# Gate and up products of the feed-forward network as 2 x 2 block products, three k-tile pairs of eight with seven products, on weight blocks of four k tiles

## The chip, the cores and the metric

The kernel runs on one core of one Trainium2 chip. The metric is device time in microseconds of one execution, the median of the runs shown. Inputs and output lie in HBM; the host only lays the weights out in another order before the launch.

## What is computed

The reference is a two-layer decoder trunk over 256 tokens of width 2048 in float32: layer A has a gMLP mixer, layer B a sparse-attention mixer on a shared K/V set, and each layer goes on with a SwiGLU network and a gated per-layer embedding. What the change touches is the SwiGLU network, with an inner width of 5632:

```python
def swiglu(h, w_in, w_out):
    g, u = jnp.split(h @ w_in, 2, axis=-1)
    return (jax.nn.silu(g) * u) @ w_out
# in each of the 2 layers:
x = x + swiglu(rmsnorm(x, norm_ffn[i]), ffn_w_in[i], ffn_w_out[i])
```

## The kernel before, in words

**Number format.** Every float32 operand is split into a high part in the fp32r format and the exact rest (`split`, L81: ScalarE copies the high part, VectorE subtracts it from the source). A product of two such operands is three matmuls into one PSUM bank (`mm3`, L90: high x high L91, high x rest L92, rest x high L93). Activations are the stationary operand (128 x 128), weights the moving one (128 x 512).

**Weight stream.** `wblock` (L109) loads two k tiles by 512 columns, 512 KB, into one of four `raw` tiles on the SyncE queue and splits them into one of four pairs `wh`, `wl` (128 x 1024). `gemm_blocks` (L121) makes one step for each such block: for both token tiles and both k tiles an `mm3`, 12 matmuls. All large matrices of the kernel use this stream.

**Feed-forward.** `ffn` (L328) goes over 11 chunks of 512 inner columns in three parts (4, 4 and 3 chunks). For a chunk, `gemm` makes the gate (`g`, two PSUM banks of `ps_acc`, one for each token tile), ScalarE applies Silu to it (L338), a second `gemm` makes the up half (`u`), VectorE multiplies the two (`ac`, L342), and `mid_T` (L189) turns the result around with eight TensorE transposes (`mT`, L196) and splits it into `aT`. After each part, four `fo` products with the output matrix are added to the residual in `x_sb` (L187). I call the work of one chunk up to `aT` a unit: 2 x 16 k tiles x 2 token tiles x 3 = 192 matmuls and 8 transposes. There are 11 units in each of two layers, 22 in all.

**Activations of the feed-forward.** `x_chunk_T` (L160) transposes 512 columns of the residual after each `ao` (layer A, L311 to L322) or `bo` (layer B, L703 to L717) chunk, and splits them with the norm's gain into `hT`. The row norms are applied later, as a scale `rs` at the Silu and at the multiplication.

**Buffers.** PSUM has eight banks: four in `ps_acc` (`gemm_acc`) and four in `ps_gen` (transposes and small products). Scratch tiles `t0`, `t1`, `t2` have two buffers each.

**Order of the work.** Each engine runs its own instructions in a fixed order. That order is laid by the scheduler of the tile framework when the program is built, from the order of the source, the dependences and its own estimate of the durations; an instruction can be put ahead of one that stands earlier in the source. The SyncE queue takes the weight loads in source order; `issue_after` puts the few other loads behind them. After the `ao` chunk 2 that queue also writes a replicated bias table of 4.2 MB (`prepare_bias`, L230).

Of the kernel before, what the change touches and what calls it, by code (L numbers as in the profile page):

```python
# [17 lines left out]
TT = 2  # L18
# [31 lines left out]

@with_exitstack
def trunk_kernel(ctx: ExitStack, tc: tile.TileContext, a: dict, out: bass.AP):
# [4 lines left out]
    wp = ctx.enter_context(tc.tile_pool(name="wp", bufs=4))  # L57
# [36 lines left out]

    def gen_bank(nm):
        return ps_gen.tile([P, NC], F32, tag="gen", name=nm)

    def rsqrt_mean(dst, ss, n):
        """dst = (ss / n + EPS) ** -0.5"""
        w = ss.shape[-1]  # L100
        ms = sm.tile([P, 16], F32, tag="ms", name="ms")
        pr = ss.shape[0]
        nc.vector.tensor_scalar(ms[:pr, :w], ss, 1.0 / n, EPS, op0=ALU.mult, op1=ALU.add)
        nc.gpsimd.tensor_tensor(dst, ms[:pr, :w], neg_half[:pr, :w], ALU.pow)

# [1 line left out]
    last_load = [None]  # L107

    def wblock(src, off, n):  # L109
        raw = wp.tile([P, KT * NC], F32, tag="raw", name="raw", bufs=4)  # L110
        sz = P * KT * n
        last_load[0] = nc.sync.dma_start(raw[:, :KT * n], src[off:off + sz].rearrange("(p f) -> p f", p=P))
        wh = wp.tile([P, KT * NC], F32R, tag="wh", name="wh")
        wl = wp.tile([P, KT * NC], F32R, tag="wl", name="wl")
        split(wh[:, :KT * n], wl[:, :KT * n], raw[:, :KT * n])
        return wh, wl

    def gemm_acc(nm):
        return [ps_acc.tile([P, NC], F32, tag="acc", name=f"{nm}_{t}") for t in range(TT)]

    def gemm_blocks(accs, acth, actl, src, off, n, nk):  # L121
        """one closure for each KT k tiles of a chunk whose blocks start at element off"""
        def block(b):
            wh, wl = wblock(src, off + b * P * KT * n, n)
            for t in range(TT):
                cs = slice(t * P, (t + 1) * P)
                for j in range(KT):
                    k = b * KT + j
                    mm3(accs[t][:, :n], acth[:, k, cs], actl[:, k, cs],
                        wh[:, j * n:(j + 1) * n], wl[:, j * n:(j + 1) * n],  # L130
                        start=(k == 0), stop=(k == nk - 1))
        return [lambda b=b: block(b) for b in range(nk // KT)]

    def weave(blocks, side):
        """the blocks in order, with the side steps spread between them"""
        done = 0
        for i, blk in enumerate(blocks):
            blk()
            upto = len(side) * (i + 1) // len(blocks)
            for st in side[done:upto]:  # L140
                st()
            done = upto
# [17 lines left out]
    def x_chunk_T(dst, which, c):  # L160
        """transposed, gained and split columns of x for the next matmul"""
        hi, lo = dst
        for kk in range(0, 4, 2):
            pt = gen_bank("xT")
            for j in range(2):
                k = c * 4 + kk + j
                for t in range(TT):
                    nc.tensor.transpose(pt[:, j * SEQ + t * P:j * SEQ + (t + 1) * P],
                                        x_sb[:, t, k * P:(k + 1) * P], ident)
            for j in range(2):  # L170
                k = c * 4 + kk + j
                split(hi[:, k, :], lo[:, k, :], pt[:, j * SEQ:(j + 1) * SEQ], gain(which, k))

# [30 lines left out]
    # ================= layer A: gMLP mixer =================  # L204
# [25 lines left out]
    def prepare_bias(pool, tbl, oh):  # L230
        """bias_rep[p, h, m]: the masked bias of head h at distance 255 - m, the same for each p"""
# [11 lines left out]
    with ExitStack() as actx:  # L243
# [31 lines left out]
        for c in range(NCH):  # L275
# [7 lines left out]
            # keep s <= t (partition s, column t)  # L283
# [28 lines left out]
    hT = big_pair("h", "hF0")  # L312
    ss = new_ss()
    with tc.tile_pool(name="prep", bufs=1) as prep:
        for c in range(NCH):
            accs = gemm(f"ao{c}", gT[0], gT[1], a["a_w_out"], c * CH_D, NC, KD)
            add_to_x(accs, c)
            x_chunk_T(hT, G_FFN0, c)
# [3 lines left out]
            if c == 2:  # L322
                prepare_bias(prep, *onehot)

    def ffn(layer, hT, ss, which_next):
# [6 lines left out]
        for pi, part in enumerate(parts):  # L332
            aT = big_pair("big", f"aT{layer}_{pi}")
            for ci, c in enumerate(part):
                accg = gemm(f"g{c}", hT[0], hT[1], win, c * CH_D, NC, KD)
                sil = tp.tile([P, TT, NC], F32, tag="t0", name="sil")
                for t in range(TT):
                    nc.scalar.activation(sil[:, t, :], accg[t], AF.Silu, scale=rs[:, t:t + 1])  # L338
                accu = gemm(f"u{c}", hT[0], hT[1], win, (FCH + c) * CH_D, NC, KD)
                ac = tp.tile([P, TT, NC], F32, tag="t1", name="ac")  # L340
                for t in range(TT):
                    nc.vector.scalar_tensor_tensor(ac[:, t, :], accu[t], rs[:, t:t + 1], sil[:, t, :],  # L342
                                                   op0=ALU.mult, op1=ALU.mult)
                mid_T(aT, ci * 4, ac)
# [46 lines left out]
    rs = finish_rstd(ss2)  # L391

    # ================= shared K/V and layer B: NSA mixer =================
    with ExitStack() as bctx:
# [27 lines left out]
                # T holds for each l [high part | rest] of 30 columns: one pass gives both rows  # L422
# [56 lines left out]
        # selected and window branches: k | v  # L479
# [27 lines left out]
        # compressed branch: k_c | v_c  # L507
# [40 lines left out]
        def attn_steps(h, qh, ql, e):  # L548
            """the steps of one head; softmax rows are ordered S1 W1 S0 W0 C1 C0 (branch, token tile)"""
# [3 lines left out]
            def scores():  # L553
# [7 lines left out]
                # bias[p, c]: distance 128 + p - c; the keys of the compressed branch end 16 apart  # L561
# [18 lines left out]
                for r, (lv, sv_, bv) in enumerate(rows):  # L580
                    # lv = -(score + bias), nmx = -max(score + bias)
# [13 lines left out]
            def transposes():  # L595
# [3 lines left out]
                for b in range(2):  # L599
# [3 lines left out]
                    # only the first 16 rows of these two are used  # L603
# [81 lines left out]
        for h0, nh, n, c0 in Q_CHUNKS:  # L685
# [3 lines left out]
            # steps between the blocks of the next chunk: each finds its inputs ready  # L689
# [13 lines left out]
        hT = big_pair("h", "hF1")  # L703
        ss = new_ss()
        acc2 = [gemm_acc(f"bo{c}") for c in range(2)]
        blk2 = [gemm_blocks(acc2[c], oT[0], oT[1], a["b_w_out"], c * CH_D, NC, KD) for c in range(2)]
        weave(blk2[0][:6] + blk2[1][:6], side)
        for c in range(NCH):
            if c < 2:
                accs = acc2[c]  # L710
                for blk in blk2[c][6:]:
                    blk()
            else:
                accs = gemm(f"bo{c}", oT[0], oT[1], a["b_w_out"], c * CH_D, NC, KD)
            add_to_x(accs, c)
            x_chunk_T(hT, G_FFN1, c)
            x_chunk_stats(ss, c)  # L717
# [7 lines left out]
    ple(1, hT, ss, store)  # L725


# [1 line left out]
def _tiled(w, widths=None):  # L729
    """[K, N] -> flat: per chunk of columns, per KT k tiles, [128, KT, n]"""  # L730
# [12 lines left out]

def _buckets(dist):
    """T5 buckets of the relative positions (a table of the shapes alone)"""
# [19 lines left out]
def _layout(i):  # L765
# [35 lines left out]
    for n in ("ffn_w_in", "ffn_w_out", "ple_w", "ple_gate"):  # L801
        r[n] = np.stack([_tiled(A[n][l]) for l in range(2)])
# [18 lines left out]
```

## Time and profile before

| | us |
|---|---|
| median of 3 runs | 2315.26 |
| lowest, highest run | 2313.7, 2316.68 |
| the profiled execution, first to last instruction | 2313.6 |
| TensorE busy in it (matmuls) | 2293.5 (99%) |
| VectorE busy in it | 1267.5 (55%) |
| ScalarE busy in it | 1107.5 (48%) |

The page gives the span of the profiled execution and no other time of it; the median of the runs is 1.7 us above that span. Busy times are unions over an engine's instructions. A matmul's own duration is not its cost in a stream, since matmuls overlap; the distance from one to the next is.

### The profile page before, as it was taken

The numbers are of one execution on the slowest core, as the hardware profiler recorded it, in microseconds if no ns is written. First come the engines' busy times: TensorE is split into PE (matmuls) and PEld (weight loads), VectorE is DVE, ScalarE is ACT, GpSimd is POOL, SyncE is SP. The second block draws the span as 40 slices with busy tenths as digits, with TensorE's granted clock in tenths as the row PEclk, the third lists the DMA queues.
The fourth block names the chain that finished last, engine by engine and source line by source line (L and its number), as shares of the span: only waits on it lengthen the run. The fifth ranks groups of instructions, "written<-read, shape, count | busy, mean of one in ns | idle before, by whom it ended". The sixth has DMA issues, their size and how long they took to land.

```text
span 2313.6 us, 27764 instructions
## 1 busy us (share of the span) xinstructions
PE 2293.5 (99%) x10617; PEld 1903.5 (82%) x10617; DVE 1267.5 (55%) x1587; ACT 1107.5 (48%) x1471; POOL 23.9 (1%) x26
## 2 busy tenths in 40 slices
PE   8999999999999999999999999999999999999999
PEld 6888878888888888888887998888888888888887
DVE  5565554454454545555667776545545445444654
ACT  6554454443444344455557665544434443344543
POOL 0000000000000000000000000000000000000000
PEclk9999999999999999999999999999999999999999
DMA  8665675565655665556657344565555556555564
GB/s 291 188 194 180 214 237 190 191 191 191 191 190 184 195 195 184 190 186 187 183 176 239 114 149 137 183 196 184 190 194 190 190 191 191 192 190 191 187 197 149
DMA packets 122882, 438.63 MB, mean 190 GB/s; under 512 B 13708, under 2 KB 15884, under 8 KB 122237
## 3 DMA queue, kind: packets, MB, share of 16 engines
q1 hardware_dynamic: 121372, 434.40, 58.9%
q10 hardware_dynamic: 1296, 2.20, 0.3%
q8 instruction: 83, 1.36, 0.2%
q14 instruction: 51, 0.41, 0.1%
q0 software_dynamic: 80, 0.26, 0.0%
HBM read 434.68 MB, written 6.46 MB: 191 GB/s over the span
## 4 chain that ended last, share of the span: by engine, by line
PE 96%; DMA 2%; DVE 1%; ACT 1%; issue 0%; POOL 0%; SPq 0%; DVEq 0%; ACTq 0%
PE u L91 8%; PE u L93 8%; PE u L92 8%; PE fo L91 7%; PE fo L92 7%; PE fo L93 7%; PE g L92 7%; PE g L93 7%; PE g L91 7%; PE pg L91 2%; PE pg L93 2%; PE pg L92 2%; PE bo L91 1%; PE bo L93 1%; PE bo L92 1%; PE mT L196 1%
## 5 line engine op out<-in xcount | busy, mean ns | idle before, releaser
L85 DVE TENSOR_TENSOR wl<-raw,wh 128x1024 fp32r<-128x1024 f32 (+1 forms) x808 | 980.8, 1216 | 971.7 <-ACT wh L84 971.2
L84 ACT ACTIVATE wh<-raw 128x1024 fp32r<-128x1024 f32 (+1 forms) x808 | 849.4, 1053 | 1097.7 <-PE u L93 313.0
L91 PE MATMUL g<-wh,hF0h 128*128 128x512 f32 x352 | 137.3, 390 | 1.3 <-ACT wh L84 1.3
L92 PE MATMUL g<-wl,hF0h 128*128 128x512 f32 x352 | 137.9, 392 | 0.5 <-DVE wl L85 0.5
L92 PE MATMUL g<-wl,hF1h 128*128 128x512 f32 x352 | 137.8, 392 | 0.0
L93 PE MATMUL g<-wh,hF1l 128*128 128x512 f32 x352 | 137.8, 391 | 0.0
L93 PE MATMUL g<-wh,hF0l 128*128 128x512 f32 x352 | 137.7, 391 | 0.0
L91 PE MATMUL g<-wh,hF1h 128*128 128x512 f32 x352 | 137.2, 390 | 0.0
L91 PE MATMUL u<-wh,hF0h 128*128 128x512 f32 x352 | 136.9, 389 | 0.0
L92 PE MATMUL u<-wl,hF0h 128*128 128x512 f32 x352 | 136.9, 389 | 0.0
L93 PE MATMUL u<-wh,hF0l 128*128 128x512 f32 x352 | 136.9, 389 | 0.0
L91 PE MATMUL u<-wh,hF1h 128*128 128x512 f32 x352 | 136.9, 389 | 0.0
L92 PE MATMUL u<-wl,hF1h 128*128 128x512 f32 x352 | 136.9, 389 | 0.0
L93 PE MATMUL u<-wh,hF1l 128*128 128x512 f32 x352 | 136.9, 389 | 0.0
L93 PE MATMUL fo<-wh,aT_0l 128*128 128x512 f32 x256 | 99.8, 390 | 0.0
L93 PE MATMUL fo<-wh,aT_1l 128*128 128x512 f32 x256 | 99.8, 390 | 0.0
L92 PE MATMUL fo<-wl,aT_0h 128*128 128x512 f32 x256 | 99.8, 390 | 0.0
L92 PE MATMUL fo<-wl,aT_1h 128*128 128x512 f32 x256 | 99.8, 390 | 0.0
L91 PE MATMUL fo<-wh,aT_1h 128*128 128x512 f32 x256 | 99.6, 389 | 0.0
L91 PE MATMUL fo<-wh,aT_0h 128*128 128x512 f32 x256 | 99.6, 389 | 0.0
L91 PEld LDWEIGHTS g<-wh,hF0h 128*128 128x128 f32 x352 | 66.0, 188 | 15.2 <-ACT wh L84 1.7
L92 PEld LDWEIGHTS g<-wl,hF0h 128*128 128x128 f32 x352 | 66.1, 188 | 14.3 <-DVE wl L85 1.0
(272 smaller groups left out, 4181.2 us busy)
## 6 DMA issues: line engine op xcount, KB each, us to landing
raw<-in_ffn_w_in SPq DMA_DIRECT2D x352, 512.0 KB, 3.5
raw<-in_ffn_w_out SPq DMA_DIRECT2D x176, 512.0 KB, 3.5
raw<-in_a_w_in SPq DMA_DIRECT2D x64, 512.0 KB, 4.0
raw<-in_ple_gate SPq DMA_DIRECT2D x64, 512.0 KB, 3.6
raw<-in_a_w_out SPq DMA_DIRECT2D x32, 512.0 KB, 3.6
raw<-in_b_w_out SPq DMA_DIRECT2D x32, 512.0 KB, 3.5
raw<-in_kv_w SPq DMA_DIRECT2D x24, 512.0 KB, 3.7
raw<-in_b_w_in SPq DMA_DIRECT2D x24, 384.0 KB, 3.5
```

The source lines that it names most:

```text
L84: nc.scalar.activation(hi, src, AF.Copy)
L85: nc.vector.tensor_tensor(lo, src, f32v(hi), ALU.subtract)
L91: nc.tensor.matmul(ps, lh, rh, start=start, stop=False)
L92: nc.tensor.matmul(ps, lh, rl, start=False, stop=False)
L93: nc.tensor.matmul(ps, ll, rh, start=False, stop=stop)
L196: nc.tensor.transpose(pt[:, j * SEQ + t * P:j * SEQ + (t + 1) * P], src[:, t, (kk + j) * P:(kk + j + 1) * P], ident)
```

## The change

The gate and up halves of one chunk are made together in `ffn_unit`. For a pair of k tiles (a, b), the activations of the two token tiles form a 2 x 2 block matrix, and the four weight blocks (up and gate of k tiles a and b) another. In five pairs of eight (0, 1, 3, 5, 7), the eight block products are kept. In pairs 2, 4 and 6 Strassen's scheme (Winograd's form) takes seven products, of sums of the blocks. Products gather over all pairs in seven PSUM banks (four of `ps_acc`, three of `ps_gen`), and the gate and up chunks are sums of these banks. So that plain pairs can use the same banks, one token tile's product with the up half takes the difference of the activations (`extra`).

The weight of a pair, 1 MB, is now one block. `ffn_w_in` is laid out so on the host (`_paired`). The weight stream is opened anew for stretches: narrow as before, or wide, with blocks of four k tiles (128 x 2048) in three buffers of each kind. It is wide from `ao` to the end of the first embedding step and from the last quarter of `bo` chunks 0 and 1 to the end. It is narrow in the gMLP's first matrix and in the attention.

```diff
+NPAIR = KD // 2
+PAIRS7 = (2, 4, 6)
...
-    wp = ctx.enter_context(tc.tile_pool(name="wp", bufs=4))
...
+    def open_stream(wide):
+        cur["sb"] = es = ExitStack()
+        cur["kt"] = 2 * KT if wide else KT
+        cur["nblk"] = 0
+        for nm in ("raw", "wh", "wl"):
+            cur[nm] = es.enter_context(tc.tile_pool(name="w_" + nm, bufs=2 if wide else 4, reuse_waits="tile"))
+        cur["third"] = es.enter_context(tc.tile_pool(name="w_third", bufs=1, reuse_waits="tile")) if wide else None
+        return es
...
+    def x_chunk_forms(dst, which, c):
+        hi, lo, exh, exl = dst
+        for j in (2 * c, 2 * c + 1):
...
+            f = tp.tile([P, 8, P], F32, tag="t2", name="f")
+            for i in range(2):
+                nc.scalar.activation(f[:, 2 * i:2 * i + 2, :].rearrange("p t s -> p (t s)"),
+                                     pt[:, i * SEQ:(i + 1) * SEQ], AF.Copy, scale=gain(which, k + i))
+            if j in PAIRS7:
...
+                nc.vector.tensor_tensor(s3, a0, a1, ALU.subtract)
+                nc.vector.scalar_tensor_tensor(a1, a1, -1.0, b1, op0=ALU.mult, op1=ALU.subtract)
+                nc.vector.scalar_tensor_tensor(s2, a1, -1.0, a0, op0=ALU.mult, op1=ALU.subtract)
+                nc.vector.tensor_tensor(s4, b0, s2, ALU.subtract)
+                ne = 3
+            else:
+                nc.vector.tensor_tensor(f[:, 4:6, :], f[:, 0:4:2, :], f[:, 1:4:2, :], ALU.subtract)
+                ne = 2
...
+            split(exh[:, e:e + ne, :], exl[:, e:e + ne, :], f[:, 4:4 + ne, :])
...
+    def ffn_unit(c, forms, win, rs):
...
+        for j in order:
+            ka, kb, e = 2 * j, 2 * j + 1, EX_OFF[j]
+            raw = wraw(win, (c * NPAIR + j) * P * 4 * NC, 4, NC)
...
+            if j in PAIRS7:
+                t13 = tp.tile([P, 2, NC], F32, tag="t2", name="t13")
+                nc.vector.tensor_tensor(t13, r[:, 1:3], r[:, 0:1].to_broadcast([P, 2, NC]), ALU.subtract)
+                t24 = tp.tile([P, 2, NC], F32, tag="t2", name="t24")
+                nc.vector.tensor_tensor(t24[:, 0], r[:, 2], t13[:, 0], ALU.add)
+                nc.vector.tensor_tensor(t24[:, 1], r[:, 3], t24[:, 0], ALU.subtract)
+                split(wh[:, NC:], wl[:, NC:], raw[:, NC:])
+                prod(1, j, plain(ka, 0), wh, wl, 1, j == last[1])
+                prod(2, j, plain(kb, 0), wh, wl, 3, j == last[2])
+                prod(3, j, extra(e + 2), wh, wl, 2, j == last[3])
+                wh, wl = wpair(nsplit[0])
+                nsplit[0] += 1
+                for i, t in enumerate((t13, t24)):
+                    split(wh[:, 2 * i * NC:2 * (i + 1) * NC], wl[:, 2 * i * NC:2 * (i + 1) * NC],
+                          t.rearrange("p s n -> p (s n)"))
+                prod(6, j, extra(e), wh, wl, 2, j == last[6])
+                prod(7, j, extra(e + 1), wh, wl, 1, j == last[7])
+                prod(4, j, plain(kb, 1), wh, wl, 3, j == last[4])
+                prod(5, j, plain(ka, 1), wh, wl, 0, j == last[5])
+            else:
+                split(wh, wl, raw)
+                for b, slots in ((2, (1, 3)), (4, (1, 3)), (5, (0, 2)), (3, (0, 2))):
+                    for i, s in enumerate(slots):
+                        form = extra(e + i) if b == 3 else plain(ka + i, 0 if b == 2 else 1)
+                        prod(b, j, form, wh, wl, s, j == last[b] and i == 1)
+        A = tp.tile([P, TT, NC], F32, tag="t0", name="gt")
+        B = tp.tile([P, TT, NC], F32, tag="t1", name="up")
+        add = lambda o, b, i: nc.vector.tensor_tensor(o, bank[b], i, ALU.add)
+        nc.scalar.activation(A[:, 0], bank[1], AF.Copy)
+        add(B[:, 0], 6, A[:, 0])
+        add(B[:, 1], 7, B[:, 0])
+        add(A[:, 0], 2, A[:, 0])
+        nc.scalar.activation(A[:, 0], A[:, 0], AF.Silu, scale=rs[:, 0:1])
+        add(A[:, 1], 4, B[:, 1])
+        nc.scalar.activation(A[:, 1], A[:, 1], AF.Silu, scale=rs[:, 1:2])
+        add(B[:, 1], 5, B[:, 1])
+        add(B[:, 0], 5, B[:, 0])
+        nc.vector.scalar_tensor_tensor(B[:, 1], B[:, 1], rs[:, 1:2], A[:, 1], op0=ALU.mult, op1=ALU.mult)
+        add(B[:, 0], 3, B[:, 0])
+        nc.vector.scalar_tensor_tensor(B[:, 0], B[:, 0], rs[:, 0:1], A[:, 0], op0=ALU.mult, op1=ALU.mult)
+        return B
...
-                accg = gemm(f"g{c}", hT[0], hT[1], win, c * CH_D, NC, KD)
...
-                accu = gemm(f"u{c}", hT[0], hT[1], win, (FCH + c) * CH_D, NC, KD)
...
+                mid_T(aT, ci * 4, ffn_unit(c, hT, win, rs))
```

## Rows read from the trace of the kernel before

**Rows 1.** The page: the span, the engines' busy time (us, share of the span, instructions), and the shares by engine of the chain of work that ended last.

```profile
span 2313.6 us, 27764 instructions
PE 2293.5 (99%) x10617; PEld 1903.5 (82%) x10617; DVE 1267.5 (55%) x1587; ACT 1107.5 (48%) x1471; POOL 23.9 (1%) x26
PE 96%; DMA 2%; DVE 1%; ACT 1%; issue 0%; POOL 0%; SPq 0%; DVEq 0%; ACTq 0%
```

**Rows 2.** What TensorE waited for, over the whole span: total us, times, the longest in us; the longest entries.

```profile
PE v L91 <- ACT wh L84: 9.2, 2, 7.4
PE g L91 <- ACT wh L84: 1.3, 1, 1.3
...
PE g L92 <- DVE wl L85: 0.5, 1, 0.5
```

**Rows 3.** Busy time by stretch (from:to in us, its length, then busy us and instructions of TensorE, weight loads, VectorE, ScalarE, GpSimd; granted clock, DMA share, GB/s): one unit of layer A, the `fo` products after the first part, and the stretch with the attention.

```profile
381.90:426.50 44.60, 44.60 (x202) 36.73 (x202) 22.16 (x21) 19.36 (x21) 0.00 (x0) 1.00 0.61 188
...
472.00:602.00 130.00, 130.00 (x578) 107.71 (x576) 64.73 (x59) 52.23 (x51) 0.00 (x0) 1.00 0.60 193
...
1205.00:1450.00 245.00, 241.93 (x1391) 212.78 (x1390) 180.25 (x451) 160.42 (x366) 9.76 (x6) 1.00 0.51 162
```

**Rows 4.** The chain that ended last, in order of time (start us, duration us, what): the first transposes of the first four units.

```profile
337.37 0.34 PE mT L196 x2
338.18 0.66 PE mT L196 x6
381.97 0.34 PE mT L196 x2
...
426.54 0.34 PE mT L196 x2
...
471.10 0.34 PE mT L196 x2
```

**Rows 5.** The instructions in order of time (start us, duration us), ScalarE alone, in a run of `u` blocks; in brackets the idle time before and what ended it.

```profile
376.11 1.06 ACT L84 ACTIVATE wh<-raw 128x1024 fp32r<-128x1024 f32 x1 [1.66 <-PE u L93]
378.83 1.06 ACT L84 ACTIVATE wh<-raw 128x1024 fp32r<-128x1024 f32 x1 [1.66 <-PE u L93]
381.55 1.06 ACT L84 ACTIVATE wh<-raw 128x1024 fp32r<-128x1024 f32 x1 [1.66 <-PE u L93]
```

**Rows 6.** Groups of instructions by line and shape over the whole span: count, busy us, mean ns of one, idle us before.

```profile
L85 DVE TENSOR_TENSOR wl<-raw,wh 128x1024 fp32r<-128x1024 f32 x776 | 950.1, 1225 | 961.5 <-ACT wh L84 961.0
L84 ACT ACTIVATE wh<-raw 128x1024 fp32r<-128x1024 f32 x776 | 821.9, 1060 | 1072.6 <-PE u L93 313.0 <-PE fo L93 277.7 <-PE g L93 239.0
...
L342 DVE SCALAR_TENSOR_TENSOR ac<-u,rstd,sil 128x512 f32<-128x512 f32 x44 | 30.9, 743 | 0.0
L187 DVE TENSOR_TENSOR x_sb<-fo,x_sb 128x512 f32<-128x512 f32 x48 | 30.8, 682 | 0.0
...
L85 DVE TENSOR_TENSOR wl<-raw,wh 128x768 fp32r<-128x768 f32 x24 | 22.5, 949 | 4.8 <-ACT wh L84 4.8
...
L84 ACT ACTIVATE wh<-raw 128x768 fp32r<-128x768 f32 x24 | 20.2, 844 | 18.7 <-PE q L93 17.2 <-DMA raw<-in_b_w_in 0.7 <-DVE pbl L85 0.5
...
L85 DVE TENSOR_TENSOR aT_0l<-mT,aT_0h 128x512 fp32r<-128x512 f32 x16 | 10.3, 684 | 0.0
```

**Rows 7.** The instructions in order of time around the end of a unit in layer A (start us, duration us), all engines.

```profile
646.40 1.40 DVE L342 SCALAR_TENSOR_TENSOR ac<-u,rstd,sil 128x512 f32<-128x512 f32 x2
646.46 0.39 PE L93 MATMUL u<-wh,hF0l 128*128 128x512 f32 x1
...
646.69 0.39 PE L91 MATMUL g<-wh,hF0h 128*128 128x512 f32 x1
...
647.20 0.44 PE L196 MATMUL mT<-ident,ac 128*128 128x128 f32 x2
...
647.98 1.22 DVE L85 TENSOR_TENSOR wl<-raw,wh 128x1024 fp32r<-128x1024 f32 x1 [0.17 <-ACT wh L84]
```

**Rows 8.** DMA issues by line: count, KB of each, median us from issue to landing.

```profile
raw<-in_ffn_w_in SPq DMA_DIRECT2D x352, 512.0 KB, 3.5
...
bias_rep<-d SPq DMA_DIRECT2D x1, 4224.0 KB, 18.6
...
x_sb<-in_x SPq DMA_DIRECT2D x2, 1024.0 KB, 7.2
```

**Rows 9.** Busy time by stretch, columns as in Rows 3, near the start of the kernel.

```profile
28.00:32.00 4.00, 3.52 (x16) 2.59 (x14) 0.55 (x2) 1.88 (x6) 0.00 (x0) 1.00 1.02 413
32.00:34.00 2.00, 0.67 (x2) 0.30 (x2) 0.69 (x1) 2.00 (x6) 0.00 (x0) 1.00 0.53 207
34.00:36.00 2.00, 1.47 (x6) 1.15 (x6) 1.66 (x2) 2.00 (x4) 0.00 (x0) 0.83 0.39 59
36.00:40.00 4.00, 4.00 (x14) 3.17 (x13) 3.04 (x6) 3.90 (x8) 0.42 (x1) 0.66 0.81 251
40.00:44.00 4.00, 4.00 (x19) 3.31 (x18) 1.09 (x2) 3.99 (x7) 0.29 (x1) 1.00 1.03 380
```

More of the change, by code (lines that the diff above doesn't have):

```diff
@@ L48 @@
 G_MIX0, G_FFN0, G_PLE0, G_KV, G_MIX1, G_FFN1, G_PLE1 = range(7)
+NPAIR = KD // 2
+PAIRS7 = (2, 4, 6)
+PAIRS8 = tuple(j for j in range(NPAIR) if j not in PAIRS7)
+EX_OFF = {}
+for _j in range(NPAIR):
+    EX_OFF[_j] = sum(3 if _i in PAIRS7 else 2 for _i in range(_j))
+EX_N = 3 * len(PAIRS7) + 2 * len(PAIRS8)
 @with_exitstack
@@ L93, in mm3, with wtile, acc_bank @@
         nc.tensor.matmul(ps, ll, rh, start=False, stop=stop)
+    cur = {}
+    def open_stream(wide):
[6 more added lines that the diff above has]
+        return es
+    def wtile(nm, dt, i):
+        pool = cur["third"] if cur["third"] is not None and i % 3 == 2 else cur[nm]
+        return pool.tile([P, cur["kt"] * NC], dt, tag=nm, name=nm)
+    def acc_bank(nm):
+        return ps_acc.tile([P, NC], F32, tag="acc", name=nm)
     def gen_bank(nm):
@@ L107, in trunk_kernel, with wraw, wpair, wblock @@
     last_load = [None]
[L109 to L115, printed above, removed]
+    def wraw(src, off, kt, n):
+        i = cur["nblk"]
+        cur["nblk"] += 1
+        raw = wtile("raw", F32, i)
+        sz = P * kt * n
+        last_load[0] = nc.sync.dma_start(
+            raw[:, :kt * n].rearrange("p (b f) -> p b f", f=KT * n),
+            src[off:off + sz].rearrange("(b p f) -> p b f", p=P, f=KT * n))
+        return raw
+    def wpair(i):
+        return wtile("wh", F32R, i), wtile("wl", F32R, i)
+    nsplit = [0]
+    def wblock(src, off, n, kt=KT):
+        raw = wraw(src, off, kt, n)
+        wh, wl = wpair(nsplit[0])
+        nsplit[0] += 1
+        split(wh[:, :kt * n], wl[:, :kt * n], raw[:, :kt * n])
         return wh, wl
     def gemm_acc(nm):
[L119 to L124, printed above, removed]
+        return [acc_bank(f"{nm}_{t}") for t in range(TT)]
+    def gemm_blocks(accs, acth, actl, src, off, n, nk, k0=0):
+        def block(kb, kt):
+            wh, wl = wblock(src, off + kb * P * n, n, kt)
             for t in range(TT):
                 cs = slice(t * P, (t + 1) * P)
-                for j in range(KT):
-                    k = b * KT + j
+                for j in range(kt):
+                    k = kb + j
                     mm3(accs[t][:, :n], acth[:, k, cs], actl[:, k, cs],
@@ L131, in block @@
                         start=(k == 0), stop=(k == nk - 1))
-        return [lambda b=b: block(b) for b in range(nk // KT)]
+        return [lambda kb=kb: block(kb, min(cur["kt"], nk - kb)) for kb in range(k0, nk, cur["kt"])]
     def weave(blocks, side):
@@ L172, in x_chunk_T, with new_forms @@
                 split(hi[:, k, :], lo[:, k, :], pt[:, j * SEQ:(j + 1) * SEQ], gain(which, k))
+    def new_forms(pool, nm):
+        return big_pair("h", nm) + (pool.tile([P, EX_N, P], F32R, tag="exh", name="exh"),
+                                    pool.tile([P, EX_N, P], F32R, tag="exl", name="exl"))
+    def x_chunk_forms(dst, which, c):
+        hi, lo, exh, exl = dst
+        for j in (2 * c, 2 * c + 1):
+            k = 2 * j
+            pt = gen_bank("xT")
+            for i in range(2):
+                for t in range(TT):
+                    nc.tensor.transpose(pt[:, i * SEQ + t * P:i * SEQ + (t + 1) * P],
+                                        x_sb[:, t, (k + i) * P:(k + i + 1) * P], ident)
+            f = tp.tile([P, 8, P], F32, tag="t2", name="f")
+            for i in range(2):
+                nc.scalar.activation(f[:, 2 * i:2 * i + 2, :].rearrange("p t s -> p (t s)"),
+                                     pt[:, i * SEQ:(i + 1) * SEQ], AF.Copy, scale=gain(which, k + i))
+            if j in PAIRS7:
+                a0, a1, b0, b1 = (f[:, i, :] for i in range(4))
+                s2, s3, s4 = (f[:, i, :] for i in range(4, 7))
+                nc.vector.tensor_tensor(s3, a0, a1, ALU.subtract)
[6 more added lines that the diff above has]
+                ne = 2
+            split(hi[:, k:k + 2, :].rearrange("p k s -> p (k s)"), lo[:, k:k + 2, :].rearrange("p k s -> p (k s)"),
+                  f[:, 0:4, :].rearrange("p f s -> p (f s)"))
+            e = EX_OFF[j]
+            split(exh[:, e:e + ne, :], exl[:, e:e + ne, :], f[:, 4:4 + ne, :])
     def new_ss():
@@ L202, in trunk_kernel @@
     CH_D = D * NC
+    open_stream(False)
     hT = big_pair("h", "hA")
@@ L310, in trunk_kernel @@
             mid_T(gT, c * 4, u)
-    hT = big_pair("h", "hF0")
+    cur["sb"].close()
+    fctx = open_stream(True)
+    exp = fctx.enter_context(tc.tile_pool(name="exp", bufs=1, reuse_waits="tile"))
+    hT = new_forms(exp, "hF0")
     ss = new_ss()
@@ L317, in trunk_kernel @@
             add_to_x(accs, c)
-            x_chunk_T(hT, G_FFN0, c)
+            x_chunk_forms(hT, G_FFN0, c)
             x_chunk_stats(ss, c)
@@ L323, in trunk_kernel, with prod, plain, extra @@
                 prepare_bias(prep, *onehot)
+    def ffn_unit(c, forms, win, rs):
+        hi, lo, exh, exl = forms
+        bank = {}
+        done = set()
+        order = range(NPAIR)
+        last = {b: max(j for j in order if b > 0 and (j in PAIRS7 or b in (2, 3, 4, 5))) for b in range(1, 8)}
+        assert order[-1] not in PAIRS7 or last[2] == order[-1]
+        def prod(b, j, form, wh, wl, s, stop):
+            if b not in bank:
+                bank[b] = (gen_bank if b in (1, 6, 7) else acc_bank)(f"p{b}")
+            ws = slice(s * NC, (s + 1) * NC)
+            mm3(bank[b], form[0], form[1], wh[:, ws], wl[:, ws], b not in done, stop)
+            done.add(b)
+        def plain(k, t):
+            return hi[:, k, t * P:(t + 1) * P], lo[:, k, t * P:(t + 1) * P]
+        def extra(e):
+            return exh[:, e, :], exl[:, e, :]
+        for j in order:
+            ka, kb, e = 2 * j, 2 * j + 1, EX_OFF[j]
+            raw = wraw(win, (c * NPAIR + j) * P * 4 * NC, 4, NC)
+            r = raw.rearrange("p (s n) -> p s n", n=NC)
+            wh, wl = wpair(nsplit[0])
+            nsplit[0] += 1
+            if j in PAIRS7:
[8 more added lines that the diff above has]
+                prod(3, j, extra(e + 2), wh, wl, 2, j == last[3])
+                wh, wl = wpair(nsplit[0])
+                nsplit[0] += 1
+                for i, t in enumerate((t13, t24)):
[27 more added lines that the diff above has]
+        return B
@@ L334, in ffn @@
             for ci, c in enumerate(part):
-                accg = gemm(f"g{c}", hT[0], hT[1], win, c * CH_D, NC, KD)
-                sil = tp.tile([P, TT, NC], F32, tag="t0", name="sil")
-                for t in range(TT):
-                    nc.scalar.activation(sil[:, t, :], accg[t], AF.Silu, scale=rs[:, t:t + 1])
-                accu = gemm(f"u{c}", hT[0], hT[1], win, (FCH + c) * CH_D, NC, KD)
[L340 to L344, printed above, removed]
+                mid_T(aT, ci * 4, ffn_unit(c, hT, win, rs))
             last = pi == len(parts) - 1
@@ L391, in trunk_kernel @@
     rs = finish_rstd(ss2)
+    fctx.close()
+    open_stream(False)
     with ExitStack() as bctx:
@@ L701, in trunk_kernel @@
             side += [tr, va]
-        hT = big_pair("h", "hF1")
-        ss = new_ss()
         acc2 = [gemm_acc(f"bo{c}") for c in range(2)]
[L706 to L717, printed above, removed]
+        blk2 = [gemm_blocks(acc2[c], oT[0], oT[1], a["b_w_out"], c * CH_D, NC, KD)[:6] for c in range(2)]
+        weave(blk2[0] + blk2[1], side)
+    cur["sb"].close()
+    fctx = open_stream(True)
+    exp = fctx.enter_context(tc.tile_pool(name="exp", bufs=1, reuse_waits="tile"))
+    hT = new_forms(exp, "hF1")
+    ss = new_ss()
+    for c in range(NCH):
+        if c < 2:
+            accs = acc2[c]
+            blks = gemm_blocks(accs, oT[0], oT[1], a["b_w_out"], c * CH_D, NC, KD, 12)
+        else:
+            accs = gemm_acc(f"bo{c}")
+            blks = gemm_blocks(accs, oT[0], oT[1], a["b_w_out"], c * CH_D, NC, KD)
+        weave(blks, [])
+        add_to_x(accs, c)
+        x_chunk_forms(hT, G_FFN1, c)
+        x_chunk_stats(ss, c)
     hT, ss = ffn(1, hT, ss, G_PLE1)
@@ L725, in trunk_kernel @@
     ple(1, hT, ss, store)
+    fctx.close()
 def _tiled(w, widths=None):
@@ L741, in _tiled, with _paired @@
     return flat
+def _paired(w):
+    import numpy as np
+    K, N = w.shape
+    w = w.reshape(K // (2 * P), 2, P, 2, N // 2 // NC, NC)[:, :, :, ::-1]
+    return np.ascontiguousarray(w.transpose(4, 0, 1, 2, 3, 5)).reshape(-1)
 def _buckets(dist):
@@ L800, in _layout @@
     r["b_w_out"] = _tiled(A["b_w_out"][0])
-    for n in ("ffn_w_in", "ffn_w_out", "ple_w", "ple_gate"):
+    r["ffn_w_in"] = np.stack([_paired(A["ffn_w_in"][l]) for l in range(2)])
+    for n in ("ffn_w_out", "ple_w", "ple_gate"):
         r[n] = np.stack([_tiled(A[n][l]) for l in range(2)])
```

## The prediction, written before the change was run

> **What bounds the kernel now.** I read the head of the page first [rows 1]: TensorE is busy for 2293.5 of 2313.6 us, VectorE for 55% and ScalarE for 48%, and the chain that ended last is 96% TensorE. A busy matmul row can hide overlap, so next come the waits of TensorE [rows 2]: the largest entry over the whole span is 9.2 us, for the first chunk of the kernel (`v`). In a unit of the feed-forward it waits for nothing: busy 44.60 of 44.60 us, VectorE 22.16 [rows 3]. So the reader is to see a kernel whose time is the number of matmuls times their distance. A unit takes 44.57 us (381.97 to 426.54 to 471.10) [rows 4]. The distance comes from the splits: in steady state one starts each time TensorE leaves a weight buffer, so every 12 matmuls, and the starts lie 2.72 us apart [rows 5]: 0.2267 us for a matmul. 192 of them are 43.52 us; the other 1.05 us are the eight transposes (0.34 + 0.66 us [rows 4]) and small gaps.
>
> **What it removes.** In three pairs of eight, 24 matmuls become 21, so a unit has 183: 9 x 0.2267 = 2.04 us less, 42.53 us if TensorE stays gapless. 22 units give 44.9 us. No matmul or transpose is added elsewhere.
>
> **What it adds on VectorE.** Prices are linear in columns: 949 ns for 768 and 1225 for 1024 [rows 6] give 1.08 ns a column and 0.12 us fixed. The shapes 2048 and 1536 are not in the trace: 2.33 us and 1.78 us by that line; the ends for 2048 are 2.21 (columns alone) and 2.45 (two of 1024), 1% of a unit either way, so I take the line. The subtraction `t13` has one operand read twice; its bounds are 1.10 (columns alone) and 1.36 us (two of 512 at 0.68), and I take 1.23, the row of the same size. For one unit:
> - five plain pairs: 5 x 2.33 = 11.7 us;
> - three seven-product pairs, each `t13` 1.23, two additions of 512 at 0.68, a split of 1536 at 1.78 and two of 1024 at 1.23, so 6.81: 20.4 us;
> - the tail: seven bank additions at 0.68, two multiplications at 0.74, two splits of `aT` at 0.68 [rows 6]: 7.6 us.
>
> That is 39.7 us beside 42.53 us of TensorE: from 50% busy to 93%. On average VectorE still fits, and this margin of 2.8 us a unit is what the change hangs on. ScalarE's line (844 for 768, 1060 for 1024 [rows 6]) gives 1.92 us for 2048 and 1.49 for 1536: about 24 us a unit, hidden.
>
> **Where it is tight.** The load is uneven. A plain pair costs VectorE 2.33 against 5.44 us of TensorE, a seven-product pair 6.81 against 4.76. Over pairs 4 to 7 and the tail VectorE has 25.9 us, TensorE 21.4: it falls 4.5 us behind. Pairs 0 and 1 of the next unit pay back 6.2, pairs 2 and 3 another 1.1. So each unit runs up a debt of 4.5 us that a lead in finished weights must carry. With three buffers the lead is two of them: 10.88 us of matmuls if both hold plain pairs, less the 4.25 us that refilling one takes (1.92 + 2.33), 6.6 us; at worst both hold the halves of a seven-product pair, 2.04 + 2.72 us, less 3.5 (1.06 + 2 x 1.23), 1.3 us. Thus the wait of TensorE is between 0 and 4.5 - 1.3 = 3.2 us a unit (0 to 70 us in all). Below nothing it can't go, since a unit before has no gap. The nearest row is the stretch with the busiest VectorE, the attention: 74% busy, and TensorE idle for 3.07 of 245 us, 1.25% [rows 3]. I take that share of 42.53 us: 0.53 us a unit, **11.7 us** given back.
>
> **The banks.** Before, a gate product found its two accumulators free; now a unit holds four of four in `ps_acc`. Pair 7 ends its banks one after the other, six matmuls (1.36 us) apart, and pair 0 of the next unit takes them in the same order. Each is read by one addition, or two, and is wanted 4 x 1.36 = 5.4 us after it was done: a cover of some 4 us each. Cost nothing; it shows if VectorE is more than 4 us late.
>
> **The loads.** 1 MB must land each 5.3 us, the rate of before. 512 KB took 3.5 us and the 1 MB of `x_sb`, among other traffic, 7.2 [rows 8]; three buffers ahead cover both, so nothing. The bias table's write takes 18.6 us [rows 8] on the same queue, and the first gate product then waited 1.3 + 0.5 us [rows 2]. The old rings hold 4 + 3 blocks of 2.72 us ahead of TensorE, 19.0 us; the new ones 3 + 2 of 5.44, 27.2 us: **-1.8 us** (ends -1.8 and, if the larger block behind it is the later one, +3.5).
>
> **Opening the stream anew,** three times: at worst a full fill each, 1.92 + 2.33 us, 12.8 in all; at best nothing. The first wide buffer lies on two narrow ones that TensorE leaves 5.44 us before the end of the old stretch, more than the 4.25 of a fill, so I take nothing.
>
> **The activations' forms** (`x_chunk_forms`): some 2 us more on VectorE for each of eight chunks of 21.8 us of matmuls. Behind the last chunk, unit 0 needs pairs 6 and 7 only after pairs 0 to 5, 31 us later. Nothing.
>
> [...]
>
> **The sum.** 2315.3 - 44.9 + 11.7 - 1.8 = **2280 us**. I start from the median; the profiled span is 1.7 us under it, less than the runs' own spread of 3 us.
>
> **The rivals.**
> - *The debt is paid in full.* TensorE waits 1 to 2 us a unit, 22 to 44 us: most of the gain is given back, 2293 to 2310. For it: 93% with a lead that shrinks in pairs 4 to 6. Against it: `t13` and `t24` need no weight buffer, so 2.6 of the 6.8 us can be done ahead. Chance 0.18; up to the border of what can be told apart (0.2%, 4.6 us) it is still faster.
> - *It all cancels:* the wait is about 2.04 us a unit, 2311 to 2320. Chance 0.05.
> - *The tail is put ahead of the next split.* VectorE runs in a fixed order, laid from estimated durations. If the last addition (0.68), the last multiplication (0.74) and only then the split of the next unit's pair 0 (2.33) stand behind the last product, TensorE idles 3.75 us at each unit's end: 22 x (3.75 - 2.04) = +38, 2353 us. It decides from a wait of 2.04 us on. Against it: before, the gate's matmuls go on at 646.69 while the tail is worked off, and the next split runs only at 647.98 [rows 7], so the order has the next weights done before the tail. For it: there VectorE is half idle. Chance 0.11.
> - *The same with the clock.* [...] Chance 0.04. [...]
>
> **How the numbers follow.** The forecast, waits of up to 1 us a unit, has 0.62. With no wait it gives 2268.6, or 2267 with the other small ends; with 1 us a unit 2291, and with the 3.5 us of the bias write 2296. The range runs from 2267 over the first rival nearly to its end, 2308, and leaves out the others and its rim: 0.2. Faster by over 0.2% is 0.62 + 0.18 = 0.80, within it 0.05, slower 0.15.
>
> **What the changed profile would show.** Right: 198 matmuls fewer; units 42.5 to 43.5 us apart in the transposes; VectorE near 39 to 40 us in a unit and TensorE's waits for `wl` or `wh` under 1 us there; splits of 2048 near 2.3 us; clock at 1.00. The debt shows as TensorE waiting for `wl` in pairs 4 to 6, the tail as one long wait at the first product of each unit. I am wrong if `t13` or the splits of 2048 run slower than the line by a tenth (VectorE then has over 42.5 us and becomes the bound), or if the order on VectorE follows the source.

## The result: 2329.4 us, 0.6% slower, where 2280 us and faster was forecast

| | us |
|---|---|
| kernel before, median of 4 runs beside it | 2314.49 |
| changed kernel, median of 4 runs | 2329.39 (2328.34 to 2330.6) |
| ratio, 95% interval | 1.0061 [1.0046, 1.0075] |
| forecast | 2280, range 2267 to 2308 |
| the profiled execution, first to last instruction | 2326.6 |

The page of the changed kernel answers to [rows 1]: 198 matmuls fewer, and yet TensorE is busy for longer, 2301.5 us instead of 2293.5.

```profile
span 2326.6 us, 26376 instructions
PE 2301.5 (99%) x10419; PEld 1871.1 (80%) x10419; DVE 1596.1 (69%) x1783; ACT 1170.5 (50%) x1335; POOL 26.6 (1%) x26
PE 94%; DVE 2%; DMA 2%; ACT 1%; issue 1%; POOL 0%; SPq 0%; DVEq 0%; ACTq 0%
```

The next suspect is VectorE, and the waits of TensorE (total us, times, longest; they answer to [rows 2]) acquit it: no line has a feed-forward product (`p`) in it. Only openings of the weight stream (`bo`, `kv`, `ao`) are new.

```profile
PE v L102 <- ACT wh L95: 8.2, 2, 7.0
PE bo L103 <- DVE wl L96: 3.0, 2, 1.6
PE kv L102 <- ACT wh L95: 1.5, 1, 1.5
PE ao L103 <- DVE wl L96: 1.4, 1, 1.4
PE bo L102 <- ACT wh L95: 1.2, 1, 1.2
```

The second unit, in the columns of [rows 3], is gapless, with VectorE at 86%:

```profile
389.62:433.03 43.41, 43.41 (x193) 35.20 (x192) 37.45 (x35) 22.89 (x20) 0.00 (x0) 1.00 0.54 194
```

So a unit takes 43.41 us (the last unit of a part 44.59) where 42.53 us without a gap was reckoned. The splits are priced as on the line of [rows 6] or a little cheaper (2291 ns for 2048 columns, 2.33 us reckoned; 1753 for 1536, 1.78 reckoned):

```profile
L96 DVE TENSOR_TENSOR wl<-raw,wh 128x2048 fp32r<-128x2048 f32 x256 | 586.2, 2291 | 442.5 <-ACT wh L95 442.1
...
L96 DVE TENSOR_TENSOR wl<-raw,wh 128x1536 fp32r<-128x1536 f32 x66 | 115.7, 1753 | 4.2 <-ACT wh L95 4.2
...
L442 DVE TENSOR_TENSOR t<-raw 128x1024 f32<-128x1024 f32 x66 | 80.6, 1221 | 13.2 <-DMA raw<-in_ffn_w_in 13.2
```

The answer stands in a stretch that the change does not touch. In the gMLP's first matrix both kernels run the same blocks in the same order. Here are the instructions of TensorE in order of time (start us, duration us), the kernel before and then the changed one:

```profile
80.11 0.39 PE L91 MATMUL v<-wh,hAh 128*128 128x512 f32 x1
80.33 0.39 PE L92 MATMUL v<-wl,hAh 128*128 128x512 f32 x1
80.56 0.39 PE L93 MATMUL v<-wh,hAl 128*128 128x512 f32 x1
80.79 0.39 PE L91 MATMUL v<-wh,hAh 128*128 128x512 f32 x1
```

```profile
80.02 0.39 PE L103 MATMUL v<-wl,hAh 128*128 128x512 f32 x1
80.25 0.40 PE L104 MATMUL v<-wh,hAl 128*128 128x512 f32 x1
80.48 0.39 PE L102 MATMUL v<-wh,hAh 128*128 128x512 f32 x1
80.72 0.40 PE L103 MATMUL v<-wl,hAh 128*128 128x512 f32 x1
```

The reader should compare starts, not durations: 0.227 us apart before, 0.233 after (the starts are rounded to 0.01 us, so the mean over many tells more than one pair). Over the whole trace the mean distance is 226.9 ns before and 232 to 233 ns after, in every stretch outside the attention. The granted clock is 1.00 in both. What differs is where the tiles lie: the change opens the weight pools behind the scratch pools. In the built programs the high parts of the weights start at byte 116192 of each partition before and at 144288 after; the activations stay at 34272. Before, the difference is a multiple of 4096; after, it is 64 bytes short of a multiple of 512.

### The profile page after: what moved, and what is told of

It reads as the page before. It is cut to its first block, busy times and chain, and to the rows that moved or that the text cites. A ratio compares the mean times of both kernels' runs of the same rounds, so it can differ in the third digit from the quotient of the medians.

```text
span 2326.6 us, 26376 instructions
## 1 busy us (share of the span) xinstructions
PE 2301.5 (99%) x10419; PEld 1871.1 (80%) x10419; DVE 1596.1 (69%) x1783; ACT 1170.5 (50%) x1335; POOL 26.6 (1%) x26
## 4 chain that ended last, share of the span: by engine, by line
PE 94%; DVE 2%; DMA 2%; ACT 1%; issue 1%; POOL 0%; SPq 0%; DVEq 0%; ACTq 0%
PE p L103 13%; PE p L104 13%; PE p L102 13%; PE fo L102 7%; PE fo L104 7%; PE fo L103 7%; PE pg L104 3%; PE pg L102 3%; PE pg L103 3%; PE ao L103 1%; PE u L102 1%; PE u L104 1%; PE u L103 1%; PE ao L104 1%; PE ao L102 1%; PE bo L103 1%
## 5 line engine op out<-in xcount | busy, mean ns | idle before, releaser
L96 DVE TENSOR_TENSOR wl<-raw,wh 128x2048 fp32r<-128x2048 f32 (+4 forms) x486 | 891.0, 1841 | 575.5 <-ACT wh L95 574.7
L95 ACT ACTIVATE wh<-raw 128x2048 fp32r<-128x2048 f32 (+4 forms) x486 | 754.8, 1555 | 779.8 <-PE fo L104 275.5
L103 PE MATMUL p<-wl,hF1h 128*128 128x512 f32 x462 | 183.5, 397 | 0.0
L103 PE MATMUL p<-wl,hF0h 128*128 128x512 f32 x462 | 183.5, 397 | 0.0
L102 PE MATMUL p<-wh,hF1h 128*128 128x512 f32 x462 | 182.6, 395 | 0.0
L102 PE MATMUL p<-wh,hF0h 128*128 128x512 f32 x462 | 182.6, 395 | 0.0
L104 PE MATMUL p<-wh,hF1l 128*128 128x512 f32 x462 | 182.6, 395 | 0.0
L104 PE MATMUL p<-wh,hF0l 128*128 128x512 f32 x462 | 182.6, 395 | 0.0
L104 PE MATMUL p<-wh,exl 128*128 128x512 f32 x418 | 164.4, 393 | 0.0
L103 PE MATMUL p<-wl,exh 128*128 128x512 f32 x418 | 164.1, 393 | 0.0
```

The costliest lines, as they stand in the source:

```text
L102: nc.tensor.matmul(ps, lh, rh, start=start, stop=False)
L103: nc.tensor.matmul(ps, lh, rl, start=False, stop=False)
L104: nc.tensor.matmul(ps, ll, rh, start=False, stop=stop)
```

## The experiments

**Is it the place of the tiles?** Four kernels. The first moves one line of the kernel before:

```diff
-    wp = ctx.enter_context(tc.tile_pool(name="wp", bufs=4))
     tp = ctx.enter_context(tc.tile_pool(name="tp", bufs=2))
     sm = ctx.enter_context(tc.tile_pool(name="sm", bufs=2))
+    wp = ctx.enter_context(tc.tile_pool(name="wp", bufs=4))
```

> The kernel before, with the one line that opens the weight pool moved behind the scratch pools, so that the weight tiles lie at the byte addresses that they have in the changed kernel (high parts from 144288 instead of 116192 within a partition); same instructions, same order. Theory A (the distance between matmuls hangs on where the weight tiles lie): the distance rises from 0.2267 to about 0.233 us as in the changed kernel, and the time from 2314.5 by some 10,400 x 6.2 ns to about 2379 us. Theory B (the wider tiles, or the busier VectorE and ScalarE beside the matmuls, stretch them): distance 0.2267, time 2314.5. Theory C (something of that one profiled run or its clock): 2314.5 as well.

The second adds an unused tile of 64 bytes to the changed kernel:

```diff
     sm = ctx.enter_context(tc.tile_pool(name="sm", bufs=2))
+    pad2 = sm.tile([P, 16], F32, name="pad2", bufs=1)
+    nc.vector.memset(pad2, 0.0)
```

> The changed kernel with an unused tile of 64 bytes ahead of the weight pools, which moves weights and activation sums 64 bytes up, so that they have the same remainder by 512 as the activations, as in the kernel before. Theory A: the distance falls back to 0.227 us, time 2329.4 - 10,200 x 6.2 ns = about 2266 us. Theories B and C: 2329.

The third puts 32 bytes ahead of everything in the kernel before, the fourth does both in the changed one:

```diff
     x_sb = const.tile([P, TT, D], F32, name="x_sb")
+    pad = const.tile([P, 8], F32, name="pad")
+    nc.vector.memset(pad, 0.0)
```

> The kernel before with an unused tile of 32 bytes ahead of activations and weights, so that all of them start at a multiple of 512 bytes within a partition (before: 32 short of one). Theory A in its first form (only the weights' place relative to the activations counts): no change, 2314. [...] Theories B and C: 2314.

> The changed kernel with both unused tiles, so that activations, weights and activation sums all start at multiples of 512 bytes. Theory A, first form: as with the 64 bytes alone, about 2266 us. [...] Theories B and C: 2329.

| kernel | us | before beside it | ratio, interval |
|---|---|---|---|
| before, weights moved | 2369.34 | 2316.44 | 1.0232 [1.0217, 1.0247] |
| changed, 64 bytes | 2277.57 | 2316.44 | 0.9835 [0.982, 0.9849] |
| before, 32 bytes | 2314.2 | 2316.44 | 0.9996 [0.9986, 1.0005] |
| changed, 64 + 32 bytes | 2278.39 | 2316.44 | 0.9837 [0.982, 0.9853] |

Theory A in its first form (only the weights' place relative to the activations counts) holds: moving one line costs the kernel before 53 us, and 64 idle bytes win the changed one 52 us. Moving all of them by 32 bytes changes nothing (third and fourth). I had expected 64 us for the first and 63 for the second, which was too much: the product had the shorter matmuls in it, too. With the matmuls of 512 columns alone, 9168 in the first program and 8970 in the second, and 6.4 and 6.0 ns each, it is 59 and 54; what is missing from 59 is not explained here. The distance in the two decisive kernels, moved weights first, then the 64 bytes:

```profile
79.82 0.40 PE L93 MATMUL v<-wh,hAl 128*128 128x512 f32 x1
80.06 0.39 PE L91 MATMUL v<-wh,hAh 128*128 128x512 f32 x1
80.29 0.40 PE L92 MATMUL v<-wl,hAh 128*128 128x512 f32 x1
```

```profile
79.66 0.39 PE L104 MATMUL v<-wh,hAh 128*128 128x512 f32 x1
79.88 0.39 PE L105 MATMUL v<-wl,hAh 128*128 128x512 f32 x1
80.11 0.39 PE L106 MATMUL v<-wh,hAl 128*128 128x512 f32 x1
```

**The place of what against what?** One kernel moves the weights alone, by another shift in each block:

```diff
...
-        wh = wp.tile([P, KT * NC], F32R, tag="wh", name="wh")
-        wl = wp.tile([P, KT * NC], F32R, tag="wl", name="wl")
+        wh = wp.tile([P, KT * NC + 128], F32R, tag="wh", name="wh")
+        wl = wp.tile([P, KT * NC + 128], F32R, tag="wl", name="wl")
+        o = SHIFTS[nblk[0] % len(SHIFTS)] // 4
+        nblk[0] += 1
+        wh, wl = wh[:, o:o + KT * NC], wl[:, o:o + KT * NC]
...
```

> The kernel before, its weight tiles 512 bytes larger, and the place of the weights within them moved by 0, 4, 8, 16, 32, 64, 96, 128, 160, 192, 224, 256, 320, 384, 448 and 480 bytes, block after block in turn (the attention's bias tile has two buffers instead of three, for room). If the weights' place against the activations by some power of two counts (Theory A, first form), the distances between matmuls fall into classes by the shift: 0.2267 us at shift 0, about 0.233 at 448 (the place in the changed kernel, 64 bytes below), and the shifts with the same remainder by 64, 128 or 256 alike tell which power. If what counts is another distance (weights against raw blocks, or high part against rest, which keep theirs here), all 16 shifts give 0.2267.

The other moves activations and weights together by 448 bytes (the tile `pad` as above, with 112 columns).

> The kernel before with an unused tile of 448 bytes ahead of activations and weights: both then have the remainder 416 by 512, as the weights of the changed kernel. If only the place of one against the other counts: distance 0.2267, 2314 us. If the remainder of the weights by itself counts: 0.231 to 0.233 and up to 2379 us. (In the changed kernel the matmuls whose activations, too, had the remainder 416 lay 0.231 us apart, between neighbours at 0.233.)

Mean distance inside blocks of one shift, worked out from the starts in the trace of the first (311 to 384 distances each, the first two and the last of a block left out; blocks of 0 stand next to transposes, their median is 227):

```
shift, bytes  0     64    128   192   256   320   384   448
ns            228.7 228.9 233.3 233.4 227.0 229.5 232.4 233.3
shift, bytes  4     8     16    32    96    160   224   480
ns            238.1 233.1 231.3 233.3 234.2 233.7 232.1 233.0
```

Shifts that differ by 256 go together (0 and 256, 64 and 320, 128 and 384, 192 and 448, 224 and 480), and of the sixteen only 0 (in the median) and 256 reach 227. Most shifts lie between 231 and 234 ns anyway, so it is the pairs 0 and 256, 64 and 320 that carry this. At the start of a block the shift of the one before still shows: at 256 the first two distances are 232 and 228 ns in the mean, the rest 227. From the trace, two runs of matmuls, shift 256 first, then shift 4:

```profile
644.39 0.39 PE L94 MATMUL u<-wh,hF0l 128*128 128x512 f32 x1
644.62 0.39 PE L92 MATMUL u<-wh,hF0h 128*128 128x512 f32 x1
644.85 0.39 PE L93 MATMUL u<-wl,hF0h 128*128 128x512 f32 x1
```

```profile
661.99 0.40 PE L94 MATMUL g<-wh,hF0l 128*128 128x512 f32 x1
662.22 0.39 PE L92 MATMUL g<-wh,hF0h 128*128 128x512 f32 x1
662.46 0.40 PE L93 MATMUL g<-wl,hF0h 128*128 128x512 f32 x1
```

It took 2359.34 us in its one run; with both moved together by 448 the kernel takes 2314.91, with a mean distance of 226.9. So it is the place of the moving operand (weights) against the stationary one (activations) that counts. The raw blocks are out: in the kernel with the moved pool they moved with the weights, in the sweep they stayed where they were, and the distance rose in both.

One thing looks like an exception: in the changed kernel the matmuls whose activations are the sums (`exh`, `exl`) have the same remainder as their weights, and yet most of them lie 231 ns apart, not 227. Its trace settles this in part. In the seven-product pairs nine such matmuls follow one another, 66 times in all. In the mean the first six distances are 228 to 236 ns, the last three 226 to 227 (worked out from the starts). So the distance does come down to 227 at an equal remainder, but only some six matmuls after the place has changed. The scratch tiles are out by this too: their place against the weights is the same for these nine as for the matmuls around them. Why the change takes six matmuls to show, no run tells.

**What are the removed matmuls worth, and is VectorE the next bound?** Both on the version with the 64 bytes: once with no seven-product pair, once with four.

```diff
-PAIRS7 = (2, 4, 6)
+PAIRS7 = ()
...
-        nc.scalar.activation(A[:, 0], bank[1], AF.Copy)
...
+        nc.scalar.activation(A[:, 0], bank[2], AF.Silu, scale=rs[:, 0:1])
+        nc.scalar.activation(A[:, 1], bank[4], AF.Silu, scale=rs[:, 1:2])
+        nc.scalar.activation(B[:, 0], bank[5], AF.Copy)
...
```

> The changed kernel with the 64 bytes, and with eight products in all eight pairs (no seven-product pair; a unit's tail then has one bank addition instead of seven). It tells what the removed matmuls are worth by themselves. Theory of the prediction's first term (time = number of matmuls x distance): 198 matmuls more x 0.2267 = +44.9 us over the 2277.6 of the version with three such pairs, 2322 us; so wide blocks and block products alone are some 8 us slower than the kernel before. Rival (VectorE's load in the seven-product pairs costs TensorE waits): clearly less than 44.9 us more.

```diff
-PAIRS7 = (2, 4, 6)
+PAIRS7 = (0, 2, 4, 6)
```

> The changed kernel with the 64 bytes and a fourth seven-product pair (0, 2, 4, 6). By the prediction's sums VectorE then has 39.7 + 6.81 - 2.33 = 44.2 us in a unit against 41.7 of TensorE. If VectorE becomes the bound there: units of about 44 us, up to 22 x 1.8 = 40 us more than 2277.6, TensorE waiting for wl. If the output products after each part let it catch up, less of that; if VectorE's sum was too high: 22 x 3 x 0.2267 = 15 us less, 2262.6 us.

| seven-product pairs | us | ratio to before, interval |
|---|---|---|
| none | 2326.4 | 1.0045 [1.003, 1.006] |
| three (the 64 bytes) | 2277.57 | 0.9835 [0.982, 0.9849] |
| four | 2301.21 | 0.9937 [0.9921, 0.9954] |

Three pairs are worth 48.8 us against none. One unit of each, none and then three, in the columns of [rows 3], shows 44.48 and 42.37 us, 2.11 us (2.04 reckoned), 22 x 2.11 = 46.4:

```profile
380.80:425.28 44.48, 44.48 (x202) 36.79 (x202) 21.71 (x13) 18.29 (x14) 0.00 (x0) 1.00 0.56 188
```

```profile
380.16:422.53 42.37, 42.37 (x193) 35.18 (x192) 37.30 (x36) 22.89 (x20) 0.00 (x0) 1.00 0.56 198
```

The fourth pair shows where VectorE ends as cover: it costs 23.6 us instead of winning 15. Its busy time in a unit rises to 41 us, the time of a unit from 42.4 (43.5 for the last of a part) to between 42.6 and 45.2 us, and products now wait for splits:

```profile
606.11:648.77 42.66, 42.19 (x190) 34.32 (x189) 41.13 (x40) 24.25 (x21) 0.00 (x0) 1.00 0.56 197
648.77:692.47 43.70, 42.52 (x191) 34.25 (x189) 41.05 (x40) 24.26 (x21) 0.00 (x0) 1.00 0.54 193
```

```profile
PE p L104 <- ACT wh L97: 15.0, 17, 4.3
...
PE p L105 <- DVE wl L98: 5.6, 7, 1.8
```

More than half of the 23.6 us is lost in the first unit of each layer, which now begins with a seven-product pair. From its first product to its first transposes it takes 56.1 and 54.2 us, where the version with three pairs takes 48.3 and 48.1: 13.9 us in both layers. In the first of them TensorE waits 3.1 us for a split (the first row has it idle for most of 2.5 us), and the granted clock is 0.50 in the 10 us behind that (columns of [rows 3]):

```profile
297.00:299.50 2.50, 0.42 (x1) 0.19 (x1) 2.50 (x5) 2.03 (x3) 0.00 (x0) 0.99 0.00 0
299.50:309.70 10.20, 7.39 (x17) 4.81 (x17) 10.05 (x10) 3.91 (x3) 0.00 (x0) 0.50 0.48 170
```

In the second layer TensorE waits 4.3 us at once, and the clock is 0.50 from 1487.3 to 1490.7 us. So the loss is in part the splits and in part, behind the waits, the clock.

**Where are the other 10 us?** 22 units give 22 x (44.57 - 42.37) = 48.4 us, the run with the 64 bytes only 38.9. By the two traces, the feed-forward and the gated embedding behind it take 47.6 us less in the two layers, as the units say, but the stretch from the first `bo` product to the first unit takes 10.0 more. Its chain in order of time shows the second wide opening: ScalarE begins the first wide split at 1391.16, as the last narrow block is done, VectorE follows, and the `bo` matmuls behind it lie 0.43 us apart, twice the usual, at half the clock (0.51 granted, last row).

```profile
1342.25 0.43 PE bo L104
...
1385.00 6.16 issue
1391.16 1.92 ACT wh L97
1393.11 2.30 DVE wl L98
1395.46 0.80 PE bo L105
1396.25 0.43 PE bo L106
...
1462.68 0.74 PE xT L234 x6
```

```profile
1400.00:1405.00 5.00, 5.00 (x15) 4.03 (x14) 0.69 (x1) 0.60 (x1) 0.00 (x0) 0.51 0.96 390
```

From the first `bo` matmul to the last transposes this is 120.4 us; the same two points of the kernel before are 110.8 apart:

```profile
1366.08 0.43 PE bo L91
...
1476.92 0.66 PE xT L168 x6
```

The built program says why: the narrow buffers are used in the order 0, 3, 2, 1, and the first wide tile lies on 0 and 1, so on the one used last. One kernel makes the `bo` chunks 0 and 1 wholly in the narrow stream:

```diff
-        blk2 = [gemm_blocks(acc2[c], oT[0], oT[1], a["b_w_out"], c * CH_D, NC, KD)[:6] for c in range(2)]
-        weave(blk2[0] + blk2[1], side)
+        blk2 = [gemm_blocks(acc2[c], oT[0], oT[1], a["b_w_out"], c * CH_D, NC, KD) for c in range(2)]
+        weave(blk2[0][:6] + blk2[1][:6], side)
+        weave(blk2[0][6:] + blk2[1][6:], [])
...
-            blks = gemm_blocks(accs, oT[0], oT[1], a["b_w_out"], c * CH_D, NC, KD, 12)
+            blks = []
```

> The changed kernel with the 64 bytes, and with the output chunks 0 and 1 of the attention (bo) made wholly in the narrow stream, so that it is opened wide behind all attention steps. In the version with the 64 bytes the first wide weight tile lies on the one that the last narrow block uses, and TensorE then waits while two splits of 2048 columns are made (3.0 + 1.2 us for bo), followed by a stretch at the half clock; from the first bo matmul to the last bo transposes it takes 120.4 us, the kernel before 110.8. Theory (what is missing from the gain is lost where the wide stream is opened): some of the 9.6 us come back, since fewer steps lie between, but the first tile is still late by a split: 2268 to 2275 us. Rival (the bo stretch is slower for another reason, such as the wide blocks in it): 2277.6.

It took 2272.92 us beside 2316.15: 0.9816 [0.9799, 0.9832], with 1.0 + 0.9 us of `bo` waits. The next one also starts each wide stretch with the third buffer:

```diff
-        cur["nblk"] = 0
+        cur["nblk"] = 2 if wide else 0
+        if wide:
+            nsplit[0] = 2
```

> As the one before, and each wide stretch begins with the third buffer, which lies outside the narrow stream's tiles and is free earlier. Theory: the waits at both openings go (1.4 us for ao, 4.2 us for bo and the half clock behind it, some 2 + 9.6 us in the chain): 2264 to 2268 us, 48 to 52 us under the kernel before. Rival: as for the one before, 2275 to 2278.

It took 2276.82 us, 0.983 [0.9815, 0.9844], where 2264 to 2268 was expected: a miss, with a time that the rival named, but not for the rival's reason. The `bo` waits are gone, as expected. At `ao`, however, the third buffer is late, and the matmuls behind it run at half clock (0.50 granted from 202 to 208 us):

```profile
PE ao L104 <- ACT wh L97: 4.2, 1, 4.2
PE ao L105 <- DVE wl L98: 2.1, 1, 2.1
```

The last one keeps the good half of both:

```diff
     fctx = open_stream(True)
+    cur["nblk"] = nsplit[0] = 2
     exp = fctx.enter_context(tc.tile_pool(name="exp", bufs=1, reuse_waits="tile"))
     hT = new_forms(exp, "hF1")
```

> The changed kernel with the 64 bytes and the bo chunks 0 and 1 in the narrow stream, the third buffer first only at the second wide opening (bo chunk 2), and ao opened as in the change. With the third buffer first at both openings, bo took 110.9 us from its first matmul to its last transposes (kernel before 110.8, the version with the 64 bytes alone 120.4), but ao's first matmuls waited 4.2 + 2.1 us instead of 1.4 and were then at half clock. Theory (each opening costs what the first buffer's old owner makes it wait): ao as in the version with the 64 bytes, bo as the kernel before: 2277.6 less 9.5 = 2268 us, 2.1% under the kernel before. Rival (the gain at bo is lost again later): 2273 to 2277.

2270.09 us beside 2313.57: 0.9807 [0.9794, 0.9821]. No `bo` wait is left, and from the first `bo` matmul to the last transposes it takes 110.9 us. It is the fastest version here, 59 us under the change as made, though its interval overlaps with that of the one without the third buffer first.

## Why the prediction was wrong, point by point

- **The step that failed** is the first: "a kernel whose time is the number of matmuls times their distance", with 0.2267 us carried over to the changed kernel as if it were a constant. The number fell by 198, as reckoned, and was worth 46 to 49 us (44.9 reckoned). But the change moved the weight pools to another place, and the distance went up by 6 ns in all large products, those outside the feed-forward included: 52 us. None of the rivals held this, and none of the signs by which the prediction said it would be wrong. With the 64 bytes that undo it, 2277.57 us lies inside the range, 2 us from the forecast.
- **VectorE.** Reckoned 39.7 us a unit, measured 37.5 (the durations in that unit add up to 39.4, but back-to-back instructions overlap a little), and waits of none instead of 0.53 us a unit: the 11.7 us given back there did not exist. The lead in finished weights did carry the debt. The four-pair kernel shows how near the edge it was: one pair more costs 23.6 us. The first rival and the two in which the tail is put first did not come about; the transposes come once the next unit is under way, as before.
- **Opening the stream** was priced at nothing, on the ground that the first wide buffer lies on two that are free early. One of the two is the last in use. Over the run with the 64 bytes that is 9.6 us at `bo` (120.4 against 110.8). The experiments there bring some 4 to 8 us of it back. That the forecast comes out near 2277.57 is therefore luck in part: two wrong terms, 11.7 and 9.6 us, of about the same size.
- **The bias table**: the wait of 1.3 + 0.5 us at the first gate product [rows 2] is gone from the list, as reckoned. **Loads**: 1 MB lands in 4.9 us in the median, hidden. **Banks**: no wait for one shows.
- **The clock** fell in stretches behind waits, to 0.66 over four microseconds near the start of the kernel before ([rows 9]) and to 0.51 at `bo` in the run with the 64 bytes, but in no unit of the change (granted 1.00 from 300 to 960 us and from 1484 to 2200). So the 0.04 that the prediction gives the tail together with the clock, part of its 0.2, stands for a loss in each unit, which no run shows: from 300 to 960 us TensorE waits for nothing in the changed kernel. In the kernel with four pairs the clock was 0.50 behind the waits of 3.1 and 4.3 us at the start of each layer. It was 1.00 in the two later units shown (the longest wait from 600 to 740 us is 0.7 us).

## What to carry to other kernels

A distance between matmuls read from a trace belongs to that placement of tiles (226.9 ns before the change, 232 to 233 after it): before it is carried over to a changed kernel, look whether the change moves the operand pools, and for operands like these keep moving and stationary tiles a multiple of 256 bytes apart within a partition (227 ns at those tried here, 229 to 238 at the other shifts). When a kernel slows down in stretches that the diff does not touch, compare the starts of the same instructions there first. Where one buffer ring takes the place of another, look which old tile the first new one lies on, and when that is last read (9.6 us at `bo` here).

## What the hardware showed that I had not expected

The place of one matmul operand against the other is worth up to 5% of the distance between matmuls here: 227 ns at the multiples of 256 bytes that were tried, 229 at 64 over, 231 to 234 for most others, 238 at 4 bytes, with float32r operands of 128 x 128 and 128 x 512. VectorE's load did not slow a matmul that had its operands: VectorE was busy for 50% of a unit before and for 88% in the run with the 64 bytes, and the distance was 227 ns in both. What one operand's address does to the distance depends on the other's: with the weights moved alone it was 233 ns, with both moved by 448 bytes 226.9. Which part of the memory makes it so, no run here shows.
